# A hybrid decoder layer on one core: the accumulator of a pair is copied by ScalarE before its seventh product, and two of the four weight sums are formed by GpSimd

## The chip, the core and the metric

The kernel runs on one core of a Trainium2 chip. The core has a matrix engine (TensorE, PE in the profile, with its weight loads as PEld), a vector engine (VectorE, DVE), a scalar engine (ScalarE, ACT), GpSimd (POOL) and a queue engine (SyncE, SP). Each engine executes its own list of instructions in order and waits for the others through semaphores. Matmul results land in PSUM banks; everything else lives in SBUF. The metric is the device time of one execution in microseconds (us), lower is better.

## The reference, cut to what matters

One decoder layer over 528 tokens (16 meta tokens and 512 others), width 1024, float32. The normalised input is multiplied by one wide projection, whose columns are the queries, keys, values and gates of two branches; a softmax attention and a gated delta network run side by side; their outputs are projected, gated, merged and projected again.

```python
hn = rms_norm(h, norm_w)
proj = hn @ w_in
aq, ak, av, az, dq, dk, dv, dz, db, da, ga, gd = jnp.split(proj, offs, axis=-1)
o_a = diff_attention(qa, ka, va, lam)               # 8 heads
y_a = (o_a * jax.nn.silu(az)) @ w_branch_attn
qkv = jax.nn.silu(causal_depthwise_conv(concatenate([dq, dk, dv]), conv_w))
o_d = gated_delta_chunked(q, k, v, beta, g)          # 8 heads
y_d = (o_d * jax.nn.silu(dz)) @ w_branch_delta
merged = jax.nn.sigmoid(ga) * y_a + jax.nn.sigmoid(gd) * y_d
out = rms_norm(h + merged @ w_out, final_norm_w)
```

The results must have float32 accuracy. The kernel gets it by splitting each factor of a large product into a high part (a rounded copy) and a low part (the remainder), and adding three matmuls: high by high, high by low, low by high.

## The kernel before

**Blocks.** The projection is cut into blocks of 128 output columns, named by their part and head (`dk 2`, `ak 0`); `ORDER` lists them. A block's weights are loaded by a DMA into one of four raw tiles (`raw`, 128x1024). ScalarE writes the high part `wh` and VectorE the low part `wl` into one of three weight slots (`W`).

**Pairs.** 17 pairs of neighbouring blocks (`ak` with `av` of each head, and two blocks each of `dk`, `dv`, `dq` from head 2 on) and 8 pairs of the branch projections (`yd`, `ya`) are computed with seven half-size products instead of eight (the Winograd form of Strassen's method). With the raw tiles `a1` and `a2` of the two blocks and the halves `h0` and `h1` of each, `split_pair` forms four sums of 128x512, all on VectorE, all in place: two make the tile `st` (weights `wb`), one goes into `a2` (this completes `wc`), one into `a1` (this is `wd`). Four sets of weights then go through ScalarE (high) and VectorE (low): `wa` from `a1`, `wb` from `st`, `wc` from `a2`, and `wd`, of half the width, from `a1`.

**Products of a pair** (`pair_of_blocks`). In the order p1, p2, p6, p5, p7, p4, p3, each twelve matmuls of 128x264 (four steps of contraction by three passes). They accumulate in banks called `r`, `s`, `t` and `q`. p5 opens bank `t`; the last one, p3, adds to the same bank. In between, what p5 has left in `t` is needed for a result of the second block: ScalarE copies bank `r` after p7 into the tile `cn`, VectorE adds bank `t` and `cn` into the second block's result tile (`xp` for the delta network's blocks, `vT` for `ak` and `av`). Only then may p3 write into `t`: in the code it waits for the event `c+`.

**Scratch.** `th` is a pool of 128x512 scratch tiles; two of them lie in the tile `room3` until the pairs of the projection are done. The gates of `az` and `dz` use them for a tanh.

**What sets the order.** Every piece of work is a generator that yields what it needs: an event, a slot of a pool, or an engine. A planner (`Plan.run`) takes, step by step, the piece that could start first by its own estimates of durations (`Engine.time`), and emits it; the lists of all engines are fixed in this way before anything runs. For a sum of 512 elements these estimates are 602 ns on VectorE and 1226 ns on GpSimd. If the estimates of one piece change, the lists of all engines change behind it. Nearly every instruction is emitted by one helper, line 231, so the profile tells groups apart by the names of their tiles: `raw<-raw,st` is a sum, `wh<-raw` a high part, `wl<-raw,wh` a low part, `bank<-sumH,wh` a matmul of a pair with summed tokens, `bank<-hnH,wh` one with the tokens themselves. GpSimd's list before holds small powers, masks (affine selects) and memsets.

Of the kernel before, what the change touches and what calls it, by code (L numbers as in the profile page):

```python
# [14 lines left out]
ALU = mybir.AluOpType  # L15
# [42 lines left out]
ORDER = dense_order()  # L58
# [3 lines left out]
HALF = L // 2  # L62
# [26 lines left out]
class Plan:  # L89
# [28 lines left out]
    def done(self, event):  # L118
        self.events[event] = self.here()
# [146 lines left out]
def hybrid_block(ctx: ExitStack, tc: tile.TileContext, x, meta, wblk, wbd, wout, pcol, prow, out):  # L266
# [4 lines left out]
    spawn, done = plan.spawn, plan.done  # L271
# [29 lines left out]
    def give(kind, at=None):  # L301
        plan.give(kind, names_.index(at.tensor.name) if kind in BANKS else 0)
# [126 lines left out]
    def split_pair(n, two):  # L429

        (a1, i1), (a2, i2) = two
        h0, h1, both = slice(0, D // 2), slice(D // 2, D), slice(0, D)
        name = (ORDER[n][0], ORDER[n][1] // 2) if ORDER[n][0] in ("yd", "ya") else n
        pairs[name] = tiles = {}

        def sums():
            yield ("st",)
            yield DVE
            V.tensor_tensor(out=st[:, h0], in0=a2[:, h0], in1=a2[:, h1], op=ALU.add)
            yield DVE  # L440
            V.tensor_tensor(out=st[:, h1], in0=st[:, h0], in1=a1[:, h0], op=ALU.subtract)
            done(f"wb sum {name}")
            yield DVE
            V.tensor_tensor(out=a2[:, h0], in0=a1[:, h0], in1=a2[:, h0], op=ALU.subtract)
            done(f"wc sum {name}")
            yield f"wa {name}"
            yield DVE
            V.tensor_tensor(out=a1[:, h1], in0=a1[:, h1], in1=st[:, h1], op=ALU.subtract)
            done(f"wd sum {name}")
            if tick(f"st {name}", 2):  # L450
                give("st")

        def low(key, src, cols, which):
            wh, wl = Ws[which]
            yield DVE
            V.tensor_tensor(out=wl[:, cols], in0=src, in1=wh[:, cols].bitcast(F32), op=ALU.subtract)
            tiles[key] = wh, wl, which
            done(f"{key} {name}")
            if key == "wb":
                if tick(f"st {name}", 2):  # L460
                    give("st")
            elif key != "wa":
                plan.give("raw", i2 if key == "wc" else i1)

# [1413 lines left out]
    def pair_of_blocks(n):  # L1878

        (n0, i0), (n1, i1) = ORDER[n], ORDER[n + 1]  # L1880
        kind = "xp" if n0 == n1 else "vT"
        acc, to, which = {}, {}, {}
        tokens = slice(0, HALF), slice(HALF, L)

        def take(m):
            if m in which:
                yield f"to {m} {n}"
                return
            which[m] = None
            if kind == "vT":  # L1890
                yield "ap"
            yield (kind,)
            which[m] = plan.task.slot
            to[m] = xps[which[m]][:, 3:3 + L] if kind == "xp" else late["vT"][which[m]]
            done(f"to {m} {n}")

        def snap(key, m, tau):
            yield from take(m)
            yield ACT
            A.copy(out=to[m][:, tokens[tau]], in_=acc["r"])  # L1900
            done(f"{key} {n}")

        def snap_c():
            yield ("cn",)
            yield ACT
            A.copy(out=cn, in_=acc["r"])
            give("pd", acc["r"])
            done(f"c {n}")

        def total(m, tau, of, key, src=None):  # L1910

            yield f"{key} {n}"
            yield from take(m)
            yield DVE
            dst = to[m][:, tokens[tau]]
            V.tensor_tensor(out=dst, in0=acc[of], in1=dst if src is None else src, op=ALU.add)
            if of != "t" or m == 0:
                give("pd", acc[of])
            if of == "t":
                done(f"{key}+ {n}")  # L1920
            if src is not None and tick(f"cn {n}", 2):
                give("cn")
            if tick(f"block {m} {n}", 2):
                name, i = ORDER[n + m]
                spawn(WHOLE[name](i, which[m]), 1)

        follow = dict(p1=lambda: snap("a", 0, 0), p2=lambda: total(0, 0, "s", "a"), p6=lambda: snap("b", 0, 1), p7=snap_c,
                      p4=lambda: total(1, 0, "q", "c", cn), p3=lambda: total(0, 1, "t", "b"))
        for key, (bk, wt, hf, part) in PAIR_PRODUCTS.items():
            if key in ("p6", "p7"):  # L1930
                yield f"{'a' if key == 'p6' else 'b'} {n}"
            if key == "p4":
                spawn(total(1, 1, "t", "c", cn), -1)
            if key == "p3":
                yield f"c+ {n}"
            yield f"{wt} {n}"
            if part in of_sum:
                yield part
            wh, wl, which_w = pairs[n][wt]
            w = wh[:, 512 * hf:512 * hf + 512], wl[:, 512 * hf:512 * hf + 512]  # L1940
            fresh = bk not in acc
            if fresh:
                yield ("pd",)
            for k in range(KB // 2):
                if part in of_sum:
                    x_ = ts_h[of_sum[part]][:, k], ts_l[of_sum[part]][:, k]
                else:
                    x_ = [hn[j][:, k + KB // 2 * (part[1] == "2"), tokens[part[2] == "2"]] for j in range(2)]
                yield PE
# [295 lines left out]
```

## Time and profile before

| | |
|---|---|
| median of 3 runs | 752.92 us (752.59 to 752.99) |
| the profiled execution's own time | 751.14 us |
| its span, first to last instruction | 749.4 us |
| mean granted TensorE clock | 0.997 |
| PE busy | 735.4 us, 98% |
| VectorE busy | 629.4 us, 84% |
| ScalarE busy | 516.0 us, 69% |
| GpSimd busy | 71.8 us, 10% |

The profile shows one execution. A row of a group gives the number of instructions, their busy time together, the mean of one, and the idle time of the engine just before them with what ended it. Matmuls overlap in their pipeline, so their mean duration is longer than the distance from one to the next, and PE counts as busy through short gaps; the waits of the weight loads (PEld) show a held-up PE more sharply than PE's own. The views with a window give the busy time of each engine in a stretch.

### The profile page before, as it was taken

The numbers are of one execution on the slowest core, as the hardware profiler recorded it, in microseconds if no ns is written. First come the engines' busy times: TensorE is split into PE (matmuls) and PEld (weight loads), VectorE is DVE, ScalarE is ACT, GpSimd is POOL, SyncE is SP. The second block draws the span as 40 slices with busy tenths as digits, with TensorE's granted clock in tenths as the row PEclk, the third lists the DMA queues.
The fourth block names the chain that finished last, engine by engine and source line by source line (L and its number), as shares of the span: only waits on it lengthen the run. The fifth ranks groups of instructions, "written<-read, shape, count | busy, mean of one in ns | idle before, by whom it ended". The sixth has DMA issues, their size and how long they took to land.

```text
span 749.4 us, 14381 instructions
## 1 busy us (share of the span) xinstructions
PE 735.4 (98%) x5299; PEld 668.8 (89%) x5299; DVE 629.4 (84%) x1417; ACT 516.0 (69%) x1381; POOL 71.8 (10%) x86
## 2 busy tenths in 40 slices
PE   9999999999999999999999999999999999999996
PEld 7998988899998899998899989888988998899875
DVE  6999999899899889889989898983679879789453
ACT  6369665979974889985597997577785445546132
POOL 2202001202100301300030210000010000000001
PEclk9999999999999999999999999999999999999999
DMA  8130522215232321334032314531122343133602
GB/s 300 59 114 29 142 62 65 70 62 170 62 122 85 73 71 52 120 100 141 29 72 72 120 56 137 212 71 58 57 66 103 142 143 113 54 108 112 231 5 108
DMA packets 45432, 74.34 MB, mean 99 GB/s; under 512 B 20729, under 2 KB 25893, under 8 KB 45362
## 3 DMA queue, kind: packets, MB, share of 16 engines
q1 hardware_dynamic: 45360, 73.43, 30.8%
q8 instruction: 41, 0.67, 0.4%
q14 instruction: 29, 0.24, 0.1%
q10 hardware_dynamic: 2, 0.00, 0.0%
HBM read 67.06 MB, written 6.36 MB: 98 GB/s over the span
## 4 chain that ended last, share of the span: by engine, by line
PE 71%; ACT 12%; DVE 11%; issue 3%; DMA 2%; SPq 0%; POOL 0%; POOLq 0%; DVEq 0%; ACTq 0%
PE bank L231 68%; DVE wl L231 3%; PE psc L231 2%; ACT wh L231 2%; ACT ak L231 1%; ACT TM L231 1%; DMA raw<-in_wblk_dram 1%; DVE tmps L231 1%; DVE ts L231 1%; DMA xt<-in_x_dram 1%; DVE y L231 1%; DVE raw L231 1%; ACT MT L231 1%; DVE ast L231 1%; ACT vr L231 1%
## 5 line engine op out<-in xcount | busy, mean ns | idle before, releaser
L231 PE MATMUL bank<-hnH,wh 128*128 128x512 f32 (+4 forms) x612 | 218.1, 361 | 2.6 <-DVE vT L231 2.1
L231 PE MATMUL bank<-hnL,wh 128*128 128x512 f32 (+4 forms) x612 | 206.1, 342 | 0.0
L231 PE MATMUL bank<-hnH,wl 128*128 128x512 f32 (+4 forms) x612 | 205.8, 342 | 0.0
L231 ACT CAST wh<-raw 128x1024 fp32r<-128x1024 f32 (+1 forms) x123 | 118.0, 960 | 50.7 <-PE bank L231 45.3
L231 DVE TENSOR_TENSOR wl<-raw,wh 128x1024 fp32r<-128x1024 f32 (+1 forms) x123 | 136.8, 1113 | 16.2 <-ACT wh L231 15.8
L231 PEld LDWEIGHTS bank<-hnH,wh 128*128 128x128 f32 x612 | 114.2, 189 | 16.2 <-DVE vT L231 2.8
L231 PEld LDWEIGHTS bank<-hnH,wl 128*128 128x128 f32 x612 | 113.8, 188 | 13.9
L231 PEld LDWEIGHTS bank<-hnL,wh 128*128 128x128 f32 x612 | 114.2, 189 | 10.0
L231 PE MATMUL bank<-sumH,wh 128*128 128x264 f32 x272 | 82.4, 303 | 0.0
L231 PE MATMUL bank<-sumH,wl 128*128 128x264 f32 x272 | 77.2, 284 | 0.0
L231 PE MATMUL bank<-sumL,wh 128*128 128x264 f32 x272 | 77.1, 283 | 0.0
L231 DVE SCALAR_TENSOR_TENSOR y<-xp,pc,y 128x528 f32<-128x528 f32 (+1 forms) x72 | 54.6, 761 | 0.5 <-ACT y L231 0.3
L231 PEld LDWEIGHTS bank<-sumH,wh 128*128 128x128 f32 x272 | 51.5, 189 | 0.6 <-issue 0.2
L231 PEld LDWEIGHTS bank<-sumL,wh 128*128 128x128 f32 x272 | 51.4, 189 | 0.0
L231 PEld LDWEIGHTS bank<-sumH,wl 128*128 128x128 f32 x272 | 51.1, 188 | 0.0
L231 ACT ACTIVATE e<-psc,ast 128x144 f32<-128x144 f32 (+3 forms) x64 | 34.5, 540 | 12.5 <-DVE ast L231 11.4
L231 PE MATMUL bank<-btH,wh 128*128 128x256 f32 x128 | 36.6, 286 | 1.0 <-ACT sn L231 0.9
L231 ACT CAST wh<-st 128x1024 fp32r<-128x1024 f32 x25 | 26.2, 1047 | 15.9 <-PE bank L231 14.6
L231 PE MATMUL bank<-btH,wl 128*128 128x256 f32 x128 | 36.1, 282 | 0.0
L231 PE MATMUL bank<-btL,wh 128*128 128x256 f32 x128 | 36.1, 282 | 0.0
L231 DVE TENSOR_TENSOR wl<-st,wh 128x1024 fp32r<-128x1024 f32 x25 | 30.7, 1229 | 6.2 <-ACT wh L231 6.2
L231 PE MATMUL psc<-ak,aq 128*128 128x264 f32 (+3 forms) x160 | 29.0, 303 | 0.4 <-ACT e L231 0.4
(381 smaller groups left out, 1723.4 us busy)
## 6 DMA issues: line engine op xcount, KB each, us to landing
raw<-in_wblk_dram SPq DMA_DIRECT2D x96, 512.0 KB, 3.5
raw<-in_wout_dram SPq DMA_DIRECT2D x8, 512.0 KB, 4.9
xt<-in_x_dram SPq DMA_DIRECT2D x4, 512.0 KB, 6.6
TM<-gcd SPq DMA_DIRECT2D x8, 256.0 KB, 5.5
xr<-in_x_dram SPq DMA_DIRECT2D x8, 256.0 KB, 6.3
out_dram<-xr SPq DMA_DIRECT2D x7, 256.0 KB, 2.3
room<-scrm SPq DMA_DIRECT2D x12, 128.0 KB, 3.4
oad<-room SPq DMA_DIRECT2D x6, 256.0 KB, 2.0
```

The source lines that it names most:

```text
L231: return real(*args, **kw)
```

## The change

Two things. First, a new piece `snap_t`: as soon as p5 is done, ScalarE copies bank `t` into a scratch tile of the pool `th`; p3 now waits for this copy (event `t`), and the sum with `cn` (now `both`) is formed by VectorE from the copy, at whatever time. Second, the sum that completes `wc` and the sum that is `wd` are issued on GpSimd (`G`) instead of VectorE (`V`).

```diff
@@ split_pair, sums()
-            yield DVE
-            V.tensor_tensor(out=a2[:, h0], in0=a1[:, h0], in1=a2[:, h0], op=ALU.subtract)
+            yield POOL
+            G.tensor_tensor(out=a2[:, h0], in0=a1[:, h0], in1=a2[:, h0], op=ALU.subtract)
             done(f"wc sum {name}")
             yield f"wa {name}"
-            yield DVE
-            V.tensor_tensor(out=a1[:, h1], in0=a1[:, h1], in1=st[:, h1], op=ALU.subtract)
+            yield POOL
+            G.tensor_tensor(out=a1[:, h1], in0=a1[:, h1], in1=st[:, h1], op=ALU.subtract)
             done(f"wd sum {name}")
@@ pair_of_blocks
+        def snap_t():
+
+            yield ("th",)
+            which["t"] = plan.task.slot
+            yield ACT
+            A.copy(out=ths[which["t"]][:, 0:HALF], in_=acc["t"])
+            done(f"t {n}")
+
+        def both():
+
+            yield f"t {n}"
+            yield f"c {n}"
+            yield from take(1)
+            yield DVE
+            V.tensor_tensor(out=to[1][:, tokens[1]], in0=ths[which["t"]][:, 0:HALF], in1=cn, op=ALU.add)
+            plan.give("th", which["t"])
+            if tick(f"cn {n}", 2):
+                give("cn")
+            finished(1)
...
-        follow = dict(p1=lambda: snap("a", 0, 0), p2=lambda: total(0, 0, "s", "a"), p6=lambda: snap("b", 0, 1), p7=snap_c,
+        follow = dict(p1=lambda: snap("a", 0, 0), p2=lambda: total(0, 0, "s", "a"), p6=lambda: snap("b", 0, 1), p5=snap_t, p7=snap_c,
                       p4=lambda: total(1, 0, "q", "c", cn), p3=lambda: total(0, 1, "t", "b"))
...
             if key == "p4":
-                spawn(total(1, 1, "t", "c", cn), -1)
+                spawn(both(), -1)
             if key == "p3":
-                yield f"c+ {n}"
+                yield f"t {n}"
```

The planner lays the lists anew, so the lists of all five engines differ nearly everywhere. Two places show what the edits do in them.

The first is PE's list at the end of the second pair (blocks `ak 1` and `av 1`), where p4 (tokens `sumH2`, `sumL2`) ends and p3 (tokens `hnH`, `hnL`) begins; `psc` is a score product of the attention. Before, and then now:

```order
L231 MATMUL bank2_3_80<-sumH2_36_136,wl1_22_120 128x264
L231 MATMUL psc_177_1450<-ak_144_1214,aq_127_971 128x400 [waits DVE_49,Activation_49]
L231 MATMUL psc_177_1450<-ak_144_1214,aq_127_971 128x400 x3
L231 MATMUL bank2_3_80<-sumH2_36_136,wh1_21_119 128x264
L231 MATMUL bank5_6_83<-hnH_128,wh2_23_121 128x264 [waits DVE_49]
```

```order
L231 MATMUL bank5_6_83<-sumH2_36_136,wl1_22_120 128x264
L231 MATMUL psc_182_1477<-ak_143_1210,aq_128_970 128x264 [waits DVE_49,Activation_49]
L231 MATMUL psc_182_1477<-ak_143_1210,aq_128_970 128x264 x3
L231 MATMUL bank5_6_83<-sumH2_36_136,wh1_21_119 128x264
L231 MATMUL bank1_2_79<-hnH_128,wh2_23_121 128x264 [waits Activation_49]
```

p3's first matmul waited for VectorE and now waits for ScalarE. The copy it waits for stands in ScalarE's list ahead of a cast and of the copy `cn`, among work of the attention (`e`, `pm`). Here is that list at the same pair, before and now:

```order
L231 ACTIVATE e_166_1356,ast_164_1354<-psc_167_1363,ast_164_1354 128x272
L231 CAST wh0_19_117<-raw2_16_114 128x1024 [waits DMAHW7_49,PE_49,Activation_49]
L231 CAST pm0_91_717<-e_155_1290 128x2x16 [waits DVE_49]
L231 COPY cn_42_167<-bank4_5_82 128x264 [waits PE_49]
L231 CAST pm1_92_718<-e_165_1355 128x2x16 [waits DVE_49]
```

```order
L231 ACTIVATE e_172_1386,ast_170_1384<-psc_173_1387,ast_170_1384 128x400
L231 COPY room3_33_133<-bank1_2_79 128x264 [waits PE_49]
L231 CAST wh0_19_117<-raw2_16_114 128x1024 [waits DMAHW3_49]
L231 COPY cn_42_167<-bank4_5_82 128x264 [waits PE_49]
L231 CAST pm1_92_718<-e_160_1314 128x2x16 [waits DVE_49]
```

The row with `room3` is new: one more copy from a bank, of the size of `cn`. It is listed before the copy `cn`, so before p7's result.

The second place is GpSimd's list from the first pair to the masks of the delta network's next heads (`ts`). Before, and then now:

```order
L231 TENSOR_TENSOR sc_96_729<-sc_96_729,phalf_108 128x4 [waits DVE_49]
L231 TENSOR_TENSOR ms_99_734<-ms_99_734,phalf_108 32x1 [waits DVE_49]
L231 AFFINE_SELECT TM_105_744<-TM_105_744 128x512 [waits Activation_49] x2
L231 MEMSET ts_205_1628 99x352 [waits DMAHW5_49,DVE_49]
L231 AFFINE_SELECT ts_205_1628<-ts_205_1628 32x352 [waits Pool_49]
```

```order
L231 TENSOR_TENSOR ms_99_734<-ms_99_734,phalf_108 32x1 [waits DVE_49]
L231 TENSOR_TENSOR raw0_14_112<-raw0_14_112,st_18_116 128x512 [waits DVE_49]
L231 AFFINE_SELECT TM_105_744<-TM_105_744 128x512 [waits Activation_49] x2
L231 TENSOR_TENSOR raw0_14_112<-raw1_15_113,raw0_14_112 128x512 [waits DMAHW5_49,DMAHW6_49,DVE_49,Pool_49]
L231 TENSOR_TENSOR raw1_15_113<-raw1_15_113,st_18_116 128x512 [waits DVE_49]
L231 TENSOR_TENSOR raw1_15_113<-raw0_14_112,raw1_15_113 128x512 [waits DMAHW1_49,DMAHW2_49,DVE_49,Pool_49]
L231 TENSOR_TENSOR raw0_14_112<-raw0_14_112,st_18_116 128x512 [waits DVE_49]
L231 MEMSET ts_207_1650 99x352 [waits DMAHW5_49,DVE_49]
```

The rows `raw<-raw,raw` are the sums for `wc`, the rows `raw<-raw,st` those for `wd`; they came from VectorE's list. ScalarE's casts of `wc` and `wd` now carry a wait for GpSimd.

More of the change, by code (lines that the diff above doesn't have):

```diff
@@ L1908, in snap_c, with finished @@
             done(f"c {n}")
+        def snap_t():
[14 more added lines that the diff above has]
+            finished(1)
+        def finished(m):
+            if tick(f"block {m} {n}", 2):
+                name, i = ORDER[n + m]
+                spawn(WHOLE[name](i, which[m]), 1)
         def total(m, tau, of, key, src=None):
@@ L1916, in total @@
             V.tensor_tensor(out=dst, in0=acc[of], in1=dst if src is None else src, op=ALU.add)
[L1917 to L1920, printed above, removed]
+            give("pd", acc[of])
             if src is not None and tick(f"cn {n}", 2):
                 give("cn")
-            if tick(f"block {m} {n}", 2):
-                name, i = ORDER[n + m]
-                spawn(WHOLE[name](i, which[m]), 1)
-        follow = dict(p1=lambda: snap("a", 0, 0), p2=lambda: total(0, 0, "s", "a"), p6=lambda: snap("b", 0, 1), p7=snap_c,
+            finished(m)
+        follow = dict(p1=lambda: snap("a", 0, 0), p2=lambda: total(0, 0, "s", "a"), p6=lambda: snap("b", 0, 1), p5=snap_t, p7=snap_c,
                       p4=lambda: total(1, 0, "q", "c", cn), p3=lambda: total(0, 1, "t", "b"))
```

## The prediction

> **What bounds the kernel now.** I read the page's busy times first, then busy time by stretch, then the waits of the weight loads, and last the single rows at one wait.
>
> ```profile
> span 749.4 us, 14381 instructions
> PE 735.4 (98%) x5299; PEld 668.8 (89%) x5299; DVE 629.4 (84%) x1417; ACT 516.0 (69%) x1381; POOL 71.8 (10%) x86
> ```
>
> PE is the bound: 14.0 us of the span are all that it is not busy, and neither edit touches a matmul. Some of that lies at the start and the end. So the change can win only in the waits of PE that its work ends, and can lose wherever it makes PE wait anew. By stretch (columns: stretch, then busy PE, PEld, DVE, ACT, POOL):
>
> ```profile
> 75.00:135.00 60.00, 58.16 (x389) 52.87 (x387) 56.35 (x140) 39.65 (x97) 6.92 (x7) 1.00 0.34 93
> 215.00:250.00 35.00, 35.00 (x210) 30.89 (x209) 34.52 (x106) 19.52 (x61) 0.00 (x0) 1.00 0.27 91
> 287.00:327.00 40.00, 39.52 (x290) 36.56 (x289) 34.33 (x74) 39.34 (x128) 10.39 (x8) 1.00 0.30 94
> 327.00:347.00 20.00, 19.25 (x156) 18.59 (x154) 18.69 (x45) 14.67 (x34) 0.65 (x1) 1.00 0.37 119
> 560.00:700.00 140.00, 138.99 (x925) 126.73 (x924) 119.73 (x198) 70.76 (x108) 0.00 (x0) 1.00 0.36 120
> ```
>
> Here a second engine is full beside PE: VectorE from 75 to 135 (3.65 us idle of 60), from 215 to 250 (0.48 of 35) and from 327 to 347 (1.31 of 20), ScalarE from 287 to 327 (0.66 of 40). There a few hundred nanoseconds more on that engine reach PE. From 560 to 700, the branch projections, VectorE has 20 us spare. What the weight loads waited for:
>
> ```profile
> PEld bank L231 <- DVE vT L231: 2.8, 3, 1.0
> PEld bank L231 <- ACT sn L231: 2.4, 7, 0.7
> PEld bank L231 <- DVE tdmt L231: 1.3, 2, 1.2
> PEld bank L231 <- DVE y L231: 0.5, 1, 0.5
> PEld bank L231 <- DVE xp L231: 0.4, 1, 0.4
> ```
>
> The rows vT and xp are the waits of p3 for the sum of `t` and `cn`. The view of the tile `cn` says so (who waited for those who use it):
>
> ```profile
> L231 ACT COPY cn<-bank x17: 352/380/388, 85.1 to 469.1; 128x264 f32<-128x264 f32 x17
> L231 DVE TENSOR_TENSOR vT<-bank,cn x16: 414/427/433, 85.8 to 470.9; 128x264 f32<-128x264 f32 x16
>   PEld bank L231: 3.2, 4
> ```
>
> So 4 of the 17 pairs hold PE up at the seventh product, 3.2 us together. One of them, row by row (ScalarE, VectorE, PE):
>
> ```profile
> 344.76 0.37 ACT L231 COPY cn<-bank 128x264 f32<-128x264 f32 x1
> 344.89 1.22 DVE L231 TENSOR_TENSOR wl<-raw,wh 128x1024 fp32r<-128x1024 f32 x1
> 346.02 0.77 DVE L231 TENSOR_TENSOR vT<-bank,cn 128x264 f32<-128x264 f32 x2
> 345.36 0.28 PE L231 MATMUL bank<-sumL,wh 128*128 128x264 f32 x1
> 345.48 0.28 PE L231 MATMUL bank<-sumH,wl 128*128 128x264 f32 x1
> 346.51 0.39 PE L231 MATMUL bank<-hnH,wh 128*128 128x264 f32 x1 [0.75 <-DVE vT L231]
> 346.51 0.19 PEld L231 LDWEIGHTS bank<-hnH,wh 128*128 128x128 f32 x1 [0.96 <-DVE vT L231]
> ```
>
> Matmuls of 128x264 follow each other every 0.12 us (345.36, 345.48); p3 should have begun at 345.60 and began at 346.51. ScalarE's copy was done at 345.13. VectorE was inside a low part of 1.22 us until about 346.1 and added only then. The cover of the old wait is p4, 12 x 0.12 = 1.4 us, and copy, low part and sum together are longer.
>
> **The change part by part.** *The seventh product.* p3 now waits for a copy that can begin when p5 ends; p7 and p4 run in between, 24 x 0.12 = 2.9 us. The copy is of the size of `cn`, 0.38 us. ScalarE works in order, and the long instructions that it has most of are casts:
>
> ```profile
> L231 ACT CAST wh<-raw 128x1024 fp32r<-128x1024 f32 x98 | 102.4, 1046 | 48.5 <-PE bank L231 43.1 <-DMA raw<-in_wout_dram 2.3 <-issue 1.4
> ```
>
> Behind one whole cast the copy ends 1.05 + 0.38 = 1.4 us after p5, behind two 2.5 us, both inside 2.9. I take all 3.2 us as won; the bounds are 3.2 and nothing (the copy as late as the old sum). The sum of copy and `cn`, off the path now, keeps its price: its row of before is 0.43 us.
>
> *ScalarE's new work.* 17 copies x 0.38 = 6.5 us on an engine that is busy 516.0 of 749.4. From 85.1 to 469.1 there is one each 24 us (16 intervals), so two in the full stretch from 287 to 327, 0.76 us against 0.66 idle. I put 0.4 us on PE, from the bounds 0 and 1.5 (two such stretches passed on whole).
>
> *Waits of PE.* Its list has 522 rows with a wait, 515 before. A first matmul that waits is longer:
>
> ```profile
> L231 PE MATMUL bank<-hnH,wh 128*128 128x264 f32 x204 | 62.9, 309 | 2.6 <-DVE vT L231 2.1 <-ACT MT L231 0.2 <-DVE xp L231 0.2
> L231 PE MATMUL bank<-hnL,wh 128*128 128x264 f32 x204 | 57.9, 284 | 0.0
> ```
>
> The 204 are 51 products of four; 25 ns more in the mean, put on the first, are 0.10 us each. Seven more waits: 0.7 us (bounds 0 and 0.7).
>
> *The sums.* What leaves VectorE:
>
> ```profile
> L231 DVE TENSOR_TENSOR raw<-raw,st 128x512 f32<-128x512 f32 x25 | 17.1, 686 | 0.1
> L231 DVE TENSOR_TENSOR raw<-raw,raw 128x512 f32<-128x512 f32 x25 | 17.1, 683 | 0.0
> ```
>
> 34.2 us, 50 sums. GpSimd forms no such sum before, so its price is bounded by the nearest rows: masks of the same 128x512 that read one tile.
>
> ```profile
> L231 POOL TENSOR_SCALAR_AFFINE_SELECT TM<-TM 128x512 f32<-128x512 f32 x8 | 10.3, 1296 | 34.3 <-issue 21.5 <-ACT TM L231 12.7
> 192.25 0.70 POOL L231 TENSOR_SCALAR_AFFINE_SELECT TM<-TM 128x512 f32<-128x512 f32 x1 [3.20 <-ACT TM L231]
> ```
>
> One takes 0.70 us at best and 1.3 in the mean. A sum reads twice as much: 0.7 to 1.4 us alone, and I take 1.3. What GpSimd does while it reads costs VectorE time, as one place shows (first GpSimd's masks, then VectorE's rows inside them, then VectorE's usual durations):
>
> ```profile
> 128.16 5.49 POOL L231 TENSOR_SCALAR_AFFINE_SELECT ts<-ts 32x352 f32<-32x352 f32 x4
> 128.69 1.22 DVE L231 TENSOR_TENSOR ak<-vT,ak 64x528 fp32r<-64x528 f32 x1
> 131.07 0.68 DVE L231 SCALAR_TENSOR_TENSOR aq<-bank,aq 64x512 fp32r<-64x512 f32 x1
> 131.78 1.22 DVE L231 TENSOR_TENSOR ak<-vT,ak 64x528 fp32r<-64x528 f32 x1
> 133.03 0.57 DVE L231 TENSOR_TENSOR pm<-e,pm 128x16 fp32r<-128x16 f32 x1
> L231 DVE TENSOR_TENSOR ak<-vT,ak x16: 690/704/1251, 94.6 to 500.2; 64x528 fp32r<-64x528 f32 x16
> L231 DVE TENSOR_TENSOR pm<-e,pm 128x16 fp32r<-128x16 f32 x32 | 6.0, 197 | 0.4 <-ACT pm L231 0.2
> ```
>
> The two `ak` rows lost 0.5 us each, `pm` lost 0.37; the row that reads a bank lost nothing. That is 1.4 us of 5.49, a quarter. At that share 50 sums of 1.3 us (65 us) take 17 us from VectorE and give it 34: a net gain of 17 us there, and none of it is on PE's path by itself. It can shorten PE's other waits for VectorE, tdmt 1.3 and y 0.5, at most 1.8 us. I take a quarter, 0.4; the other end is the first rival. The Trainium skill's page "SBUF — State Buffer", section "Who interferes with whom", says that a VectorE instruction with two SBUF inputs contends with a GpSimd instruction that reads SBUF, and that the second to issue blocks until the first is finished. The place above agrees as to which rows suffer, and by the rule a sum could cost VectorE its whole length; the sum here would then be the first rival's.
>
> A sum on GpSimd also ends later: 1.3 instead of 0.68, plus up to 1.2 us if a low part of VectorE is in front of it. Queued behind it is ScalarE's cast, and behind that all of ScalarE. The cover is the slot: casts of `wh<-raw` idle 43.1 us on PE, since a slot comes free only when PE has used it, so most casts wait longer for the slot than for the sum. I price this at nothing; without the cover it is the second rival. GpSimd's own work is moved back by at most two sums, 2.6 us, and it is idle nine tenths of the span. SP's DMAs: the same loads; `raw` comes free with the low part, as before.
>
> **Sum:** -3.2 + 0.4 + 0.7 - 0.4 = -2.5 us. The profiled execution took 751.14 us, 1.7 around its span and 1.8 under the median of the runs; I carry the difference over to the median: 752.92 - 2.5 = 750.4 us.
>
> **The rivals.** *GpSimd's reads hold VectorE (slower).* From a blocked share of 0.685 / 1.3 = 0.53 on, VectorE loses more than it gave away; at a share of 1 a sum costs it 0.6 us net. The place is the three stretches in which VectorE is full, 115 us; with 25 pairs from 54.8 to 675.3,
>
> ```profile
> L231 DVE TENSOR_TENSOR st<-raw x25: 636/685/693, 54.8 to 675.3; 128x512 f32<-128x512 f32 x25
> ```
>
> one each 26 us, they hold 4.4 pairs, 9 sums, 5.4 us. With 1.1 for ScalarE and PE's waits and 3.2 won that is +3.3: 756.2 us. For it: VectorE's work there is nearly all with two SBUF inputs. Against it: the share seen is a quarter.
>
> *The waits only move (no change).* The copy, or ScalarE behind a late sum, arrives as late as VectorE did: of 3.2 won, 2.0 come back, with the 0.7 of more waits and the 0.4 nothing to speak of is left: -0.1, 752.8 us. For it: every list is laid anew on estimates that know nothing of held-up reads, and ScalarE has 0.66 us in 40 spare from 287 to 327. Against it: 2.9 us of cover where there was 1.4.
>
> *VectorE's relief arrives whole (more).* All 1.8 us of PE's other waits for VectorE go too, and ScalarE's copies and the added waits cost nothing: -5.0, 747.9 us. Against it: these waits are for products of a chain of small steps, not for a full engine.
>
> **How the numbers follow.** The runs differ by 0.4 us; I call anything within 0.2% (1.5 us) no change. Forecast 0.40, with its own range 749.2 to 751.5; waits only move 0.25; GpSimd's reads 0.20; relief whole 0.15. Faster is the forecast but for its upper edge and the last rival: 0.53; same 0.27; slower 0.20. The range goes down to 747.6, below the largest gain, and up to 755.5, into the slower case.
>
> **What would show it.** Right: no wait of PEld for VectorE's `vT` or `xp` from a bank and `cn`, and none above 0.3 us for ScalarE's copy into `room`; GpSimd's sums around 1.3 us; VectorE busy less by 10 to 25 us. Wrong: VectorE's low parts lengthened from 1.22 to over 1.8 us beside GpSimd's sums; ScalarE's casts idle for GpSimd by more than 10 us together; new waits of PE for weights. If VectorE's busy time rises, the first rival holds.

## The result, and the profile after

The changed kernel takes 772.69 us (median of 4 runs, 770.87 to 775.82); the kernel before takes 752.75 us on the same chip (751.85 to 752.99). The ratio is 1.0271, with a 95% interval of 1.0236 to 1.0307: **2.7% slower**, 19.9 us, where 2.5 us of gain was forecast. The time also lies outside the range (747.6 to 755.5) and beyond the slower rival (756.2).

The page of the changed kernel, span and busy times, then the two new groups of GpSimd (busy time and mean ns, then the idle time before them):

```profile
span 771.6 us, 14432 instructions
PE 747.0 (97%) x5299; PEld 673.7 (87%) x5299; DVE 636.7 (83%) x1367; ACT 519.9 (67%) x1398; POOL 155.3 (20%) x136
L231 POOL TENSOR_TENSOR raw<-raw,raw 128x512 f32<-128x512 f32 x25 | 45.1, 1806 | 179.7 <-DVE st L231 179.1
L231 POOL TENSOR_TENSOR raw<-raw,st 128x512 f32<-128x512 f32 x25 | 34.3, 1370 | 80.1 <-DVE wl L231 77.0
```

VectorE has 50 instructions fewer (1367 for 1417), gave away sums of 34.2 us by their own durations, and is busy 7.3 us longer (636.7 for 629.4). What made up for it are its own rows beside GpSimd's sums. The view of the tile `st` gives minimum, median and maximum in ns:

```profile
L231 DVE TENSOR_TENSOR st<-raw x25: 635/684/1202, 56.4 to 694.4; 128x512 f32<-128x512 f32 x25
L231 DVE TENSOR_TENSOR st<-st,raw x25: 659/693/1793, 57.2 to 695.3; 128x512 f32<-128x512 f32 x25
L231 POOL TENSOR_TENSOR raw<-raw,st x25: 1261/1297/1766, 68.8 to 698.3; 128x512 f32<-128x512 f32 x25
L231 DVE TENSOR_TENSOR wl<-st,wh x25: 1205/1216/2309, 73.3 to 700.1; 128x1024 fp32r<-128x1024 f32 x25
```

Medians are as before. The maxima of the second and fourth row are 1.1 and 0.9 us above those of before (693 and 1372); the 1202 of the first row lies beside a mask, and a kernel without any sum on GpSimd (run 4) has 1203 there. An undisturbed sum on GpSimd takes 1.3 us, as the prediction had it.

One such place, and how it reaches PE (the timeline of GpSimd, VectorE, ScalarE, PE; in brackets the wait and its releaser):

```profile
192.01 1.75 POOL L231 TENSOR_TENSOR raw<-raw,st 128x512 f32<-128x512 f32 x1 [2.90 <-DVE wl L231]
192.53 1.26 DVE L231 TENSOR_TENSOR pm<-e,pm 128x16 fp32r<-128x16 f32 x1
193.72 3.85 DVE L231 SCALAR_TENSOR_TENSOR y<-xp,pc,y 128x528 f32<-128x528 f32 x5
196.93 0.64 ACT L231 ACTIVATE xp<-y 128x528 f32<-128x528 f32 x1 [1.92 <-DVE y L231]
197.48 0.24 ACT L231 CAST pmT<-bank 96x128 fp32r<-96x128 f32 x1
197.77 0.33 PE L231 MATMUL bank<-vm,pmT 96*128 96x128 f32 x1 [2.03 <-ACT pmT L231]
...
411.43 0.13 DVE L231 TENSOR_TENSOR pm<-e,pm 128x16 fp32r<-128x16 f32 x1
```

`pm` has 16 columns; the one at 411.43 takes 0.13 us. Here it takes 1.26, until GpSimd's sum is over (192.01 + 1.75 = 193.76). The five steps of `y` behind it are late, ScalarE waits for them 1.92 us, its cast `pmT` is queued behind that, and PE stands 2.03 us.

Then PE loses time once more. Busy time by stretch (PE, PEld, VectorE, ScalarE, GpSimd, then the granted clock of PE):

```profile
194.00:198.00 4.00, 1.97 (x14) 1.66 (x14) 4.00 (x6) 2.08 (x5) 0.84 (x1) 1.00 0.01 2
198.00:202.00 4.00, 4.00 (x15) 3.37 (x15) 3.94 (x7) 3.95 (x14) 0.61 (x1) 0.57 0.00 0
275.00:285.00 10.00, 10.00 (x107) 9.28 (x106) 6.12 (x9) 8.52 (x20) 0.00 (x0) 0.83 0.23 80
412.00:420.00 8.00, 8.00 (x89) 7.56 (x89) 7.57 (x13) 5.82 (x20) 1.28 (x1) 0.79 0.42 134
```

For the 4 us after that wait the clock is 0.57: 4 x 0.43 = 1.7 us lost. The other two stretches lose 10 x 0.17 and 8 x 0.21, again 1.7 us each, both behind places where PE stood (at 272 and at 409). Of the 20 us these three take 5.1. In the trace of before no stretch of 5 us between 15 and 745 us has a clock under 1.00. The runs say the same: mean clock 0.987 to 0.991 in the four runs of the change, 0.995 to 0.999 before. Not all of this comes with the sums, as run 4 shows.

The places are spread over the span, also where VectorE is far from full. In the branch projections:

```profile
641.95 1.75 POOL L231 TENSOR_TENSOR raw<-raw,raw 128x512 f32<-128x512 f32 x1 [7.54 <-DVE st L231]
641.13 0.69 DVE L231 TENSOR_TENSOR st<-raw 128x512 f32<-128x512 f32 x1 [1.70 <-DMA raw<-in_wblk_dram]
641.85 0.69 DVE L231 TENSOR_TENSOR st<-st,raw 128x512 f32<-128x512 f32 x1
642.46 2.32 DVE L231 TENSOR_TENSOR wl<-raw,wh 128x1024 fp32r<-128x1024 f32 x1
644.71 0.41 DVE L231 TENSOR_TENSOR sn<-bank,sn 128x256 f32<-128x256 f32 x1
645.17 0.39 PE L231 MATMUL bank<-b2H,wh 128*128 128x256 f32 x1 [0.86 <-DVE sn L231]
```

VectorE idled 1.70 us just before, for a load, so the sum starts together with VectorE's work on the same pair. The low part takes 2.32 us instead of 1.22, `sn` comes 1.1 us late, and PE stands 0.86 us.

### The profile page after: what moved, and what is told of

It reads as the page before. It is cut to its first block, busy times and chain, and to the rows that moved or that the text cites. A ratio compares the mean times of both kernels' runs of the same rounds, so it can differ in the third digit from the quotient of the medians.

```text
span 771.6 us, 14432 instructions
## 1 busy us (share of the span) xinstructions
PE 747.0 (97%) x5299; PEld 673.7 (87%) x5299; DVE 636.7 (83%) x1367; ACT 519.9 (67%) x1398; POOL 155.3 (20%) x136
## 4 chain that ended last, share of the span: by engine, by line
PE 55%; DVE 26%; ACT 9%; issue 4%; POOL 3%; DMA 1%; POOLq 0%; DVEq 0%; ACTq 0%
PE bank L231 53%; DVE wl L231 8%; PE psc L231 2%; ACT wh L231 2%; DVE st L231 2%; DVE room L231 2%; DVE y L231 2%; DVE ts L231 2%; DVE tmps L231 2%; DVE ast L231 1%; POOL raw L231 1%; ACT TM L231 1%; POOL ts L231 1%; DVE sumL L231 1%; DVE vT L231 1%
## 5 line engine op out<-in xcount | busy, mean ns | idle before, releaser
L231 DVE TENSOR_TENSOR wl<-raw,wh 128x1024 fp32r<-128x1024 f32 (+1 forms) x123 | 142.5, 1160 | 22.9 <-ACT wh L231 22.2
L231 PE MATMUL bank<-sumH,wh 128*128 128x264 f32 x272 | 84.0, 309 | 1.7 <-ACT xp L231 1.1
L231 POOL TENSOR_TENSOR raw<-raw,raw 128x512 f32<-128x512 f32 x25 | 45.1, 1806 | 179.7 <-DVE st L231 179.1
L231 POOL TENSOR_TENSOR raw<-raw,st 128x512 f32<-128x512 f32 x25 | 34.3, 1370 | 80.1 <-DVE wl L231 77.0
L231 DVE TENSOR_TENSOR wl<-st,wh 128x1024 fp32r<-128x1024 f32 x25 | 32.6, 1305 | 2.7 <-ACT wh L231 2.7
```

What stands on the lines that cost most here:

```text
L231: return real(*args, **kw)
```

## The experiments

Twelve kernels. Times are medians; before was 752.2 us beside each of them. "The change's lists" means all five lists of the changed kernel, instruction by instruction; "the lists of before" likewise.

**1. The copy alone, planned.** All sums on VectorE; the planner lays its lists for that.

```diff
-            yield POOL
-            G.tensor_tensor(out=a2[:, h0], in0=a1[:, h0], in1=a2[:, h0], op=ALU.subtract)
+            yield DVE
+            V.tensor_tensor(out=a2[:, h0], in0=a1[:, h0], in1=a2[:, h0], op=ALU.subtract)
```

(and the same for `a1[:, h1]`)

> The copy of bank t by ScalarE alone; all four sums stay on VectorE. Theory H (GpSimd's reads hold VectorE: each sum on GpSimd costs VectorE about a whole sum at a bad moment) and theory L (the sums end later on GpSimd and ScalarE's casts are late): the copy is innocent, 749 to 753 us, with no wait of PE for the sum of t and cn. Theory O (the lists as the planner lays them anew are worse, whatever engine forms the sums): if the copy brings that order, 760 us or more.

Measured 756.53 us, ratio 1.0061 [1.0045, 1.0078]. Neither expectation held: p3's waits are gone, and the kernel is 4.3 us slower. In the profiled execution one place is large enough to account for it. The timeline of ScalarE and PE:

```profile
198.96 1.03 ACT L231 CAST wh<-raw 128x1024 fp32r<-128x1024 f32 x1
200.28 0.63 ACT L231 CAST ak<-vT 64x528 fp32r<-64x528 f32 x1
201.21 0.48 ACT L231 COPY pT<-bank 128x384 f32<-128x384 f32 x1
201.74 0.32 PE L231 MATMUL bank<-ident,pm 128*96 128x128 f32 x1 [1.12 <-ACT pT L231]
202.97 0.39 PE L231 MATMUL bank<-hnH,wh 128*128 128x264 f32 x1 [0.91 <-ACT pT L231]
```

and busy time by stretch with the clock:

```profile
190.00:200.00 10.00, 10.00 (x68) 8.86 (x65) 8.15 (x17) 10.00 (x31) 1.65 (x2) 1.00 0.04 7
203.00:207.00 4.00, 4.00 (x21) 4.00 (x22) 1.00 (x2) 3.52 (x8) 0.00 (x0) 0.57 0.37 118
```

ScalarE was full (10.00 of 10) and its copy `pT` late; by the starts of its matmuls PE lost 1.41 and 1.20 us, and then 4 x 0.43 = 1.7 us by the clock, together 4.3, as much as the difference of the medians.

**2. The sums alone, planned.** Before, with the two sums on GpSimd and no copy.

```diff
-            yield DVE
-            V.tensor_tensor(out=a2[:, h0], in0=a1[:, h0], in1=a2[:, h0], op=ALU.subtract)
+            yield POOL
+            G.tensor_tensor(out=a2[:, h0], in0=a1[:, h0], in1=a2[:, h0], op=ALU.subtract)
```

> The two sums on GpSimd alone, without the copy. H and L: all of the loss and none of the gain of the copy, 770 to 778 us. O, if the copy brings the bad order: below 762 us.

Measured 778.83 us, 1.0367 [1.0334, 1.0400], just above what was expected; VectorE busy 637.7. The sums are what makes the change slow. This kernel is 6.1 us slower than the change, which has the copy as well, although the copy alone cost 4.3: with lists laid anew for each kernel the two edits don't simply add.

**3. The change's lists, the sums executed by VectorE.** They keep their place in the order that was laid for GpSimd.

```diff
+    GV = Engine(plan, POOL, nc.vector)
...
-            G.tensor_tensor(out=a2[:, h0], in0=a1[:, h0], in1=a2[:, h0], op=ALU.subtract)
+            GV.tensor_tensor(out=a2[:, h0], in0=a1[:, h0], in1=a2[:, h0], op=ALU.subtract)
```

> The changed kernel's lists exactly, only that the 50 sums are executed by VectorE, at the place where the planner put them; VectorE has 34 us more work than its list was planned for, and nothing holds it. H and L: back to 750 to 758 us. O: the order stays, so 766 to 776 us.

Measured 760.86 us, 1.0112 [1.0090, 1.0134], between the two expectations:

```profile
PE 739.2 (97%) x5299; PEld 669.2 (88%) x5299; DVE 630.0 (83%) x1417; ACT 519.8 (69%) x1398; POOL 81.5 (11%) x86
```

**4. The change's lists, GpSimd writes and does not read.** Where a sum stood, GpSimd writes zeros for about as long. `plan.spend` lets the planner count the time of a sum, so that the lists stay; the other sum is replaced in the same way, here and in runs 5, 10 and 12.

```diff
-            G.tensor_tensor(out=a2[:, h0], in0=a1[:, h0], in1=a2[:, h0], op=ALU.subtract)
+            plan.spend(POOL, 1226.4)
+            for o, k in ((0, 512), (0, 512), (0, 256)):
+                nc.gpsimd.memset(a2[:, h0.start + o:h0.start + o + k], 0.0)
```

> The changed kernel's lists exactly, but in the place of each sum GpSimd writes zeros for about as long (512, 512 and 256 elements) and reads nothing. The sums are left out, so the weights wc and wd are wrong and the output is too; the work of the other engines is the same. H: the hold is gone and VectorE has 34 us less to do, 745 to 753 us, VectorE's rows back at their usual lengths. L: GpSimd is as late as before, 766 to 775 us. O: 766 to 775 us.

Measured 752.53 us, 1.0005 [0.9994, 1.0016]. GpSimd is as busy as in a kernel with sums, the order is the change's, ScalarE still waits for GpSimd, and the 20 us are gone:

```profile
PE 740.5 (98%) x5299; PEld 672.7 (89%) x5299; DVE 603.0 (80%) x1367; ACT 519.9 (69%) x1398; POOL 138.4 (18%) x236
```

VectorE's busy time against the change's is the hold itself: 636.7 - 603.0 = 33.7 us, 0.67 us for each of 50 sums, a share of 0.67 / 1.3 = 0.52. A sum that is late by the time that an undisturbed one takes, or a GpSimd that is merely busy, costs nothing here; the writes in a sum's place take 0.53, 0.53 and 0.31 us. Sums that VectorE lengthens further are not in this run.

Against run 3, in the same lists, the 50 sums are worth 630.0 - 603.0 = 27.0 us of VectorE's busy time, not 34.2: neighbouring rows overlap a little (above, `pm` ends at 192.53 + 1.26 = 193.79 and the next row starts at 193.72), so fewer rows save less than their durations. These 27.0 us of VectorE's own work cost 760.86 - 752.53 = 8.3 us, 0.31 us each; the 33.7 us of the hold cost 20.2, 0.60 each. So the loss is more than a fuller VectorE.

The low clock doesn't need the reads. Run 4's profiled execution has the longest such stretch of all, 10.24 x 0.49 = 5.0 us lost, and seven of its ten executions have a mean clock of 0.993:

```profile
265.46:275.70 10.24, 10.24 (x69) 9.71 (x70) 3.96 (x6) 7.72 (x19) 0.34 (x2) 0.51 0.16 51
```

**5. One tile read.** In the change's lists GpSimd copies one 128x512 tile, and then writes zeros; the sums are left out.

```diff
-            G.tensor_tensor(out=a2[:, h0], in0=a1[:, h0], in1=a2[:, h0], op=ALU.subtract)
+            plan.spend(POOL, 1226.4)
+            nc.gpsimd.tensor_copy(out=a2[:, h0], in_=a1[:, h0])
+            nc.gpsimd.memset(a2[:, h0], 0.0)
```

> The changed kernel's lists exactly; in the place of each sum GpSimd copies 512 elements (reads one tile instead of two) and then writes 512 zeros, so it is busy about as long but reads for less than half as long. The sums are left out, so the output is wrong. Theory H (the time that GpSimd spends reading is what VectorE loses): between 752.5 (no reads) and 772.7 (two reads), near 760; VectorE's busy time between 603 and 637 us, near 617. A theory in which only GpSimd's being busy or late counts: 752.5, as without reads.

Measured 754.54 us, 1.0027 [1.0013, 1.0041]; VectorE busy 611.1, 8.1 us over the kernel that only writes: 0.16 us per copy. Both lie inside the range that was expected, well below its middle (760 and 617). A short read holds VectorE a little, a sum four times as much.

**6 and 7. The copy with half of the sums, planned:** only `wd` on GpSimd, then only `wc`.

```diff
+            yield DVE
+            V.tensor_tensor(out=a2[:, h0], in0=a1[:, h0], in1=a2[:, h0], op=ALU.subtract)
...
             yield POOL
             G.tensor_tensor(out=a1[:, h1], in0=a1[:, h1], in1=st[:, h1], op=ALU.subtract)
```

> The copy, and only the sum wd on GpSimd (25 sums); the sum wc is back on VectorE. H, if each sum on GpSimd costs alike: half of the way from the copy alone (756.5) to the changed kernel (772.7), 762 to 767 us. If the loss hangs on the sum wc, which GpSimd begins just when VectorE goes on to the second sum of st: 756 to 760 us.

> The copy, and only the sum wc on GpSimd (25 sums); wd is back on VectorE. H, if each sum costs alike: 762 to 767 us. If the loss hangs on the sum wc: 768 to 774 us.

Measured 759.12 us, 1.0088 [1.0067, 1.0108], and 758.17 us, 1.0079 [1.0063, 1.0094]: only 2.6 and 1.6 us over the copy alone, where the whole change costs 16 us over it. The first lies in the band for a loss that hangs on the sum wc, the second, which has these sums, below both of its bands: neither reading holds. Each has lists of its own, so run 11 repeats the question in one set of lists.

**8. The copy in the lists of before.** The 17 copies are put into ScalarE's list without the planner's knowledge; everything else stands row for row as before. The copies go into `tn`, a tile of the pool `th` that is kept out of the pool meanwhile; the lines that hold a copy back until its place in the list are left out here.

```diff
+            if key == "p5":
+                plan.pending.append((plan.here()[0] + 300, lambda: nc.scalar.copy(out=tn, in_=acc["t"])))
...
-            V.tensor_tensor(out=dst, in0=acc[of], in1=dst if src is None else src, op=ALU.add)
+            V.tensor_tensor(out=dst, in0=tn if of == "t" and m else acc[of], in1=dst if src is None else src, op=ALU.add)
```

> The kernel before, its five lists row for row, with nothing added but the 17 copies of bank t in ScalarE's list, which the planner does not count; the sum of t and cn reads the copy. All sums on VectorE. The copy alone, planned, took 1.0061 of the time of before. Theory P (the copies themselves load ScalarE and PE waits for it): 755 to 758 us here too. Theory Q (the copies win what the prediction said, and the lists that the planner lays with them lose it again): 749 to 751.5 us, with no wait of PE for the sum of t and cn.

Measured 752.74 us, 1.0002 [0.9991, 1.0013], between the two expectations. The waits of p3 have gone and nothing was gained. The place that the prediction showed, in this kernel (VectorE, then PE):

```profile
347.10 1.23 DVE L234 TENSOR_TENSOR wl<-raw,wh 128x1024 fp32r<-128x1024 f32 x1
348.24 0.43 DVE L234 TENSOR_TENSOR vT<-room,cn 128x264 f32<-128x264 f32 x1
349.06 0.69 DVE L234 SCALAR_TENSOR_TENSOR qT<-xp,y 128x512 f32<-128x512 f32 x1
347.72 0.28 PE L234 MATMUL bank<-sumH,wl 128*128 128x264 f32 x1
347.84 0.29 PE L234 MATMUL bank<-hnH,wh 128*128 128x264 f32 x1
349.18 0.28 PE L234 MATMUL bank<-hnH,wl 128*128 128x264 f32 x1
349.81 1.16 PE L234 MATMUL bank<-qT,kT 128*128 128x128 f32 x8 [0.35 <-DVE qT L234]
```

and before:

```profile
346.85 0.69 DVE L231 SCALAR_TENSOR_TENSOR qT<-xp,y 128x512 f32<-128x512 f32 x1
348.10 1.05 PE L231 MATMUL bank<-qT,kT 128*128 128x128 f32 x8
```

p3 starts at once at 347.84, 0.12 us behind p4. But VectorE's list is the same and full, so `qT` starts 2.21 us later on this trace's clock, just as much as everything ahead of p3 does (this execution was 1.7 us late from its first loads). Before, p3's wait let VectorE get ahead, and `qT` was ready when PE came to it; now PE comes earlier and waits for `qT`. Matched matmul by matmul, this execution gains 0.60, 0.36, 0.88 and 0.92 us at the four places, 2.8 together. Within 4 us it gives back 0.36 at the second place, 0.4 at the third and 0.44 at the fourth, at the next product that needs a late row (`ao`, `qT`). The rest comes back at other places, from 123 to 481 us, the larger part of it at products that wait for rows of ScalarE (`pmT`, `TM`, `pT`).

**9. Both edits in the lists of before.** As run 8, and the 50 sums go out of VectorE's list into GpSimd's.

```diff
+    VG = Engine(plan, DVE, nc.gpsimd)
...
-            V.tensor_tensor(out=a2[:, h0], in0=a1[:, h0], in1=a2[:, h0], op=ALU.subtract)
+            VG.tensor_tensor(out=a2[:, h0], in0=a1[:, h0], in1=a2[:, h0], op=ALU.subtract)
```

> Both edits of the change without laying any list anew: the lists of before row for row, with the 17 copies put into ScalarE's and the 50 sums put out of VectorE's list into GpSimd's. The copies alone in these lists gave 752.7 us. If the holds are the whole cost: 50 sums hold VectorE 33 us as in the change, and the time is 768 to 777 us. If the lists that the planner laid anew carry half of it (the copy alone costs 4.3 us when planned, nothing in the old lists): 758 to 765 us. VectorE's busy time 633 to 640 in both, if a hold is 0.67 us whatever the lists.

Measured 764.98 us, 1.0171 [1.0151, 1.0191], at the upper edge of the second band: with the reads in both, the new lists cost 7.7 us more. VectorE busy 641.3:

```profile
PE 740.5 (97%) x5299; PEld 668.4 (88%) x5299; DVE 641.3 (84%) x1367; ACT 521.2 (68%) x1398; POOL 154.5 (20%) x136
```

**10. The same, writing only.** As run 9, with zeros written in place of the sums.

```diff
-            VG.tensor_tensor(out=a2[:, h0], in0=a1[:, h0], in1=a2[:, h0], op=ALU.subtract)
+            plan.spend(DVE, 601.7)
+            for o, k in ((0, 512), (0, 512), (0, 256)):
+                nc.gpsimd.memset(a2[:, h0.start + o:h0.start + o + k], 0.0)
```

> As the run before (lists of before, 17 copies), but the 50 sums of wc and wd are left out and GpSimd writes zeros in their place, so the pairs' results are not the reference's: VectorE's relief by 34 us without any hold, and without p3's wait. It is the most that the change could bring in these lists. Prediction's forecast and its rival of the whole relief: 747.9 to 750.4 us. Rival (PE's waits only move on, to the next product that needs a late small step): 751.5 to 753 us. VectorE's busy time 592 to 603.

Measured 750.63 us, 0.9974 [0.9962, 0.9985]: both edits without a hold are worth 1.6 us, 0.2 us short of the forecast's band.

```profile
PE 737.2 (98%) x5299; PEld 669.3 (89%) x5299; DVE 603.5 (81%) x1367; ACT 520.1 (69%) x1398; POOL 135.5 (18%) x236
```

So in one set of lists (the same but for one place near 287 us, where 21 matmuls stand in another order) the reads of 50 sums take 641.3 - 603.5 = 37.8 us of VectorE and 764.98 - 750.63 = 14.4 us of time.

Where these 14.4 us arise can be read from the two traces, from the same first to the same last matmul of each stretch. The three stretches that the prediction called full lose 6.8 us (3.64, 1.90 and 1.27), the one from 347 to 560 4.9, those from 250 to 327 2.1. From 135 to 215 and from 560 to 700, where VectorE has time and 24 of the 50 sums lie, it is 0.04 and 0.9. The branch projections in four kernels: lists of before, writing and reading (runs 10 and 9), then the change's lists, writing and reading (run 4 and the change):

```profile
559.60:699.58 139.98, 138.96 (x925) 126.71 (x923) 111.25 (x181) 69.97 (x107) 21.97 (x48) 1.00 0.36 120
572.00:712.85 140.85, 139.59 (x924) 126.49 (x923) 124.33 (x182) 71.04 (x108) 27.40 (x16) 1.00 0.37 119
559.99:700.01 140.02, 139.56 (x927) 126.91 (x925) 116.47 (x193) 77.13 (x120) 21.95 (x48) 1.00 0.36 117
572.79:718.20 145.41, 141.60 (x926) 127.13 (x925) 128.82 (x193) 76.89 (x120) 28.67 (x16) 1.00 0.35 112
```

VectorE's busy time, the third in each row, is 13.1 us longer with the reads in the lists of before and 12.4 in the change's, so it is held about as long. In the lists of before that costs 0.9 us, in those of the change 5.4.

**11. Half the reads in the change's lists.** The sums of `wd` are formed on GpSimd; those of `wc` are replaced by zeros as in run 4.

> The change's own lists; the 25 sums of wd on GpSimd as the change has them, the 25 sums of wc left out, with GpSimd writing zeros in their place. Half the reads of the change in the same lists. With no read the time was 752.5 us, with all 772.7. If the price of a hold is a fixed share (additive): 761 to 764 us. If PE and the weight slots swallow the first holds and pass on the later ones (the two halves, each in lists of its own, cost 1.6 and 2.6 us): 754 to 758 us. VectorE's busy time in both 618 to 622.

Measured 757.57 us, 1.0076 [1.0058, 1.0094]; VectorE busy 618.2. This lies in the band for a price that grows with the number of holds. The 25 sums of `wd` cost 757.57 - 752.53 = 5.0 us, those of `wc` on top of them 15.1. VectorE's own loss is close to even (15.2 and 18.5 us), so the difference arises on PE's side. Whether the second half costs more because it comes on top, or because it is the sums of `wc`, is not shown: the kernel with only `wc` read, in these lists, wasn't run. Part of the difference is the clock: the mean over the runs is 0.9935 with writes only, 0.9953 here, 0.9895 in the change. Multiplied by it, the times are 747.6, 754.0 and 764.6: 6.4 and 10.6 us. What makes the rest stays open.

**12. The branch pairs write only.** In the change's lists the 34 sums of the projection's pairs are formed on GpSimd, the 16 of the branch pairs replaced by zeros.

```diff
             yield POOL
-            G.tensor_tensor(out=a2[:, h0], in0=a1[:, h0], in1=a2[:, h0], op=ALU.subtract)
+            if not isinstance(name, tuple):
+                G.tensor_tensor(out=a2[:, h0], in0=a1[:, h0], in1=a2[:, h0], op=ALU.subtract)
+            else:
+                plan.spend(POOL, 1226.4)
+                for o, k in ((0, 512), (0, 512), (0, 256)):
+                    nc.gpsimd.memset(a2[:, h0.start + o:h0.start + o + k], 0.0)
```

> The change's own lists, and the 34 sums of the projection's pairs on GpSimd as the change has them; the 16 sums of the branch projections' 8 pairs are left out, and GpSimd writes zeros in their place (512, 512 and 256 columns), so the branches' results are not the reference's. Matched matmul by matmul, the profiled execution of the change falls 18 us behind the one in which GpSimd only writes, and about 5.4 us of that between 575 us and the end, where VectorE had 20 us of 140 to spare. Prediction's reading (a held VectorE costs only where VectorE is full): the branch pairs' holds are free, 771 to 773 us. Rival (a hold reaches PE wherever the row that is held is one that PE is close behind, spare time or not): 766 to 768.5 us. In both VectorE's busy time falls by about 10.7 us (16 sums of 0.67) to 626.

Measured 765.44 us, 1.0182 [1.0153, 1.0211], below both bands and on the rival's side; VectorE busy 624.2. The branch pairs' 16 sums cost 772.69 - 765.44 = 7.3 us, 0.45 each, although VectorE had 20 us of 140 to spare there; the projection's 34 cost 765.44 - 752.53 = 12.9, 0.38 each. In these lists a hold costs no less where VectorE has time. In the lists of before it does (0.9 us for the same 16 sums, from the traces at run 10), so this is a property of the order, not of the hold.

## Why the prediction was wrong

The 20.5 us between before and the change (752.2 and 772.69; 19.9 against the 752.75 measured beside the change) add up over three runs: both edits without a hold -1.6 (run 10), the reads +14.4 (run 9 against run 10), and the lists that the planner laid anew +7.7 (the change against run 9). Taken in the other order, the new lists cost only 1.9 without the reads (run 4 against run 10) and the reads 20.2 (the change against run 4). So 5.8 us belong to neither alone: the reads cost more in the new lists. An estimate from the runs' intervals gives these 5.8 an uncertainty of 3.3 us.

*The sums, put at -0.4: the step that failed.* Their reads cost 14.4 us in the lists of before and 20.2 in those of the change; run 4 shows that it is the reading, since the same lists with GpSimd as busy writing take 752.53. Three things were wrong in this term.

First, the blocked share. The quarter was read from one place with masks that read one tile, and carried over to sums that read two. The share is 0.52 (0.67 us of 1.3).

Second, what VectorE gives away. In busy time the sums are worth 27.0 us, not 34.2, so VectorE loses more than it gave from a share of 27.0 / 50 / 1.3 = 0.42 on, not from 0.53. It lost 33.7. By the prediction's own signs the rival *GpSimd's reads hold VectorE* is the one that came true: VectorE's busy time rose, and low parts took up to 2.3 us. But its price, 756.2, was too low by 16 us.

Third, and this the forecast and that rival share, where a loss counts. Both set lost against won microseconds of VectorE, and the rival let a loss count only in the three stretches in which VectorE was full before. In the lists of before this is right for the places with time to spare: 24 sums cost 0.9 us there, and the three stretches lost 6.8 (the rival had 5.4 net for nine sums). What the rival left out are 4.9 us from 347 to 560 and 2.1 from 250 to 327. But the change has other lists, and in these the branch pairs, with time to spare as well, lose 5.4 us in the traces and 7.3 in run 12. One row made up to 1.1 us longer at the moment when a pair's weights are formed reaches PE wherever PE follows closely (`pm` to `pmT`, `wl` to `sn`), and where that is depends on the order. Spare time that was read from the old lists is no cover in new ones. Why the old order covers the branch pairs and the new one doesn't stays open.

The rule of the Trainium skill that the prediction weighed (page "SBUF — State Buffer", section "Who interferes with whom") is borne out row by row, though in the mean VectorE loses half of a sum's time and not the whole: the same section adds that issue order decides who blocks. In the trace `pm` at 192.53 lasts until GpSimd's sum is over. In the other order it is GpSimd that waits: a sum for `wc` that starts inside VectorE's rows takes longer, most of all this one, under a series of sums and low parts of VectorE:

```profile
579.89 7.10 POOL L231 TENSOR_TENSOR raw<-raw,raw 128x512 f32<-128x512 f32 x1 [9.35 <-DVE st L231]
```

*The seventh product, put at -3.2.* The mechanism was right: the wait is gone in the change as in run 8, and the copy is never late (the view of the tile `cn` has no wait of PE any more). The price was wrong: together with its copies it is worth nothing, 1.0002 [0.9991, 1.0013]. Around all four places an engine whose rows PE needs next is full (before, busy time by stretch; PE, PEld, VectorE, ScalarE; the place at 345 us lies in the stretch from 327 to 347 that the prediction showed):

```profile
105.00:115.00 10.00, 9.45 (x68) 8.84 (x67) 9.90 (x33) 5.08 (x11) 0.00 (x0) 1.00 0.49 154
255.00:270.00 15.00, 14.80 (x185) 13.40 (x184) 11.09 (x23) 14.42 (x39) 4.04 (x5) 1.00 0.28 75
460.00:475.00 15.00, 14.18 (x113) 13.79 (x113) 14.93 (x39) 10.11 (x25) 0.00 (x0) 1.00 0.46 159
```

VectorE is busy 9.90 of 10 and 14.93 of 15 us, ScalarE at the second place 14.42 of 15. At 265 us run 8 has given back the whole 0.36 us within 4 us, at 470 us 0.44 of 0.92 within 2 us. There the rival *the waits only move* named the outcome, but not the cause: what is late is not the copy but the next row of the full engine. More than half of the 2.8 us came back farther on, mostly where PE waits for ScalarE; whether the 17 copies make these rows late wasn't tried.

*VectorE's relief, put at a quarter of 1.8.* Run 10 against run 8 has the relief without the hold: 752.74 - 750.63 = 2.1 us, somewhat over the 1.8 of the rival *relief arrives whole*. That forecast and run 10 agree in the sum (750.4 and 750.63) is a coincidence, the terms are exchanged: nothing from the seventh product with its copies, 2.1 from the relief.

*ScalarE's copies (+0.4) and seven more waits (+0.7).* In the lists of before, the copies, the waits and the seventh product together give 0.2 us (-0.7 to +1.0). They weren't measured apart.

*What had no term: the lists laid anew.* The copy costs 4.3 us when the planner lays lists for it and nothing in the old ones; the lists for both edits cost 1.9 us without the reads and 7.7 with them. In the profiled executions single places stand out where PE waits for late rows and the clock then falls: one in run 1, as large as its whole loss, one in run 3, one three times as long in run 4, and three in the change. Runs 8, 9 and 10, in the lists of before, have none between 15 and 745 us. So the new lists bring such places also without a read, and not all of the change's 5.1 us at low clock can be put down to the reads. Why the planner's order brings these places about wasn't tried; nor whether other lists would avoid them.

*A late sum, put at nothing.* Right for an undisturbed sum: run 4's writes take as long without a cost. A sum that VectorE lengthens is another matter: behind the one of 7.10 us above ScalarE's cast waited 2.41 us. Such waits are few (4.5 us in all, twice, in the change; 0.8 us, once, in run 9, which still pays 14.4 for the reads), but no run has long sums without the hold, so their share of the 20.2 us isn't measured.

None of the kernels that compute the whole layer beats the one before.

## What to carry over

Before moving work to GpSimd, ask whether it reads SBUF beside a VectorE that works on two SBUF inputs; if so, count what it holds up at the moment it runs, row by row up to PE, and not against the total that VectorE is relieved of. Before counting a wait of the bounding engine as won, look at the next product that needs the engine it waits for; if that engine is full, part of the wait can come back there. Where a planner lays all lists anew, try the edit in the old lists as well, with and without the suspected cause: here the reads cost 14 us in the old order and 20 in the new one, and the spare time seen before covered the branch pairs only in the old.

## What the runs showed of the hardware

A GpSimd sum of 128x512 with two inputs takes 1.26 to 1.30 us undisturbed and takes 0.67 us from VectorE on average; a copy of one tile of that size 0.16 us; a write nothing that can be seen (in run 10 the rows of the tile `st` take at most 0.69 us as sums and 1.23 us as low parts, as before). When a sum starts inside VectorE's rows it can itself be held for several of them (7.10 us). Even a row of 128x16 is held until the sum is over (1.26 instead of 0.13 us).

The granted clock of TensorE fell to 0.50 for 3.4 us, 1.7 us of loss (0.57 when it is read over 4 us):

```profile
198.29:201.70 3.41, 3.41 (x12) 2.83 (x12) 3.35 (x7) 3.39 (x13) 0.31 (x1) 0.50 0.00 0
```

In the change this came behind a wait of 2.03 us at 195.7, behind two of 0.71 and 1.25 at 272, and behind one of 1.06 at 409. The page "TensorE: Matmul & The Clock Gate" of the Trainium skill, Part 1, has the clock halved after at least one idle window of about 3.4 us. An estimate from the page's figure, one such window at half speed, is 3.4 x 0.5 = 1.7 us, and the loss agrees with it. The waits that brought it on were shorter here, and not each brings it on: PE stood 1.84 us up to 123.5 us, and its clock stayed at 1.00. What decides it isn't shown.

```profile
121.00:124.00 3.00, 1.16 (x8) 0.78 (x8) 2.86 (x10) 1.34 (x3) 0.91 (x1) 1.00 0.00 0
124.00:134.00 10.00, 10.00 (x65) 8.82 (x64) 8.04 (x25) 8.21 (x21) 1.43 (x3) 1.00 0.06 17
```
